# Hybrid decoder layer on one core: the opening rebuilt (how the conditioning row is spread, how the first scale is formed, which tiles start the first projection, and in which order the first loads stand)

## The chip, the cores and the metric

The kernel runs on one core of a Trainium2 chip. The metric is the device time of one execution in microseconds (us); the median of three runs is given. The core's engines run their own queues in order and wait for each other by semaphores: PE multiplies matrices, ACT (ScalarE) and DVE (VectorE) work on tiles in SBUF and PSUM, POOL does little here, and SP issues all the loads. A row "PEld" in the profile is PE loading the stationary operand.

## The reference

One layer (BATCH 1, SEQ 256, D 2048) of a decoder with two token mixers:

```python
mod = silu(c) @ ada_w + ada_b              # 6 vectors of 2048: sh1, sc1, g1, sh2, sc2, g2
h = rms_norm(x, norm1_g) * (1 + sc1) + sh1
proj = h @ w_in + b_in                     # 22 slabs of 512 columns: u, lru_gate, q, k, v, two gates
...                                        # conv + RG-LRU on u and lru_gate, windowed attention on q, k, v
merged = sigmoid(gA) * (y_lru @ w_lru_out) + sigmoid(gB) * (y_attn @ w_attn_out)
x = x + g1 * (merged @ w_o)
h2 = rms_norm(x, norm2_g) * (1 + sc2) + sh2
x = x + g2 * ((silu(gate) * up) @ w_ffn_out)
out = rms_norm(x, final_g)
```

All inputs and the output are float32. A column of `h` (a "k-tile" is 128 of the 2048 rows of the contraction) can be formed only when the shift and the scale of that k-tile are known, and each of these is a dot product of `silu(c)` with 128 columns of `ada_w`.

## The kernel before

**Layout.** Activations are kept transposed: 16 k-tiles of 128 partitions by 256 tokens. `xT` holds x in four tiles of four k-tiles. Weights come from memory in "items" of up to two k-tiles by 512 columns (128x1024 f32, 512 KB; a single k-tile is 256 KB).

**Three products for one.** For most products a weight `raw` is split into a high part (`hi`, a CAST to fp32r on ACT, L274) and a low part (`lo = raw - hi`, a subtraction on DVE, L286); h is split in the same way into `h_hi` and `h_lo` (both in `h_both`). `mm3` (L319 to L321) issues hi\*hi, hi\*low and low\*hi. One k-tile of one 512-column slab is 4 blocks of 128 columns, so 12 matmuls of 128x256; this is called a unit below. `raw` has 5 buffers, `hi` 4 (`N_HI`), `lo` 3 (`N_LO`): the `lo` of item i cannot be written before PE has finished item i-3, the `hi` of item i not before PE has finished item i-4.

**Modulation.** For k-tile kt and vector m, 128 rows of transposed `ada_w` come as two halves of 128x1024 (`aw`). A fused multiply-and-sum on DVE (L406) multiplies each with `crow`, the row silu(c) on all 128 partitions. A short instruction (L414) finishes the scale. So k-tile kt of h takes four halves (2 MB and four L406), then `x_norm` (L433), then on ACT `hx` (L445) and the CAST to `h_hi` (L448), then `h_lo` on DVE (L450). The four halves of each k-tile are named aw0, aw1, ... in the order of their loads.

**Opening.** The row c is loaded onto one partition and spread by four matmuls with one row of ones (L162); ACT applies SiLU on the way to `crow`. The scale of k-tile 0 does not go this way: `sum_first` multiplies one column of silu(c) at a time with 128 columns of `ada_w` (`ak`, 8 loads), 16 matmuls that leave one row of 128 values; the row is copied by ACT and turned into a column by a small matmul (`scT`). The sum of squares of x goes from ACT and DVE into four matmuls (`ssc`), a root, a reciprocal, two products with an identity and a matmul (`rx_ps`), so that 1/rms stands in every partition (`rx`). Before all that, four matmuls on ones (`warm`) run on PE.

**First projection.** The slabs of `START` (8 of u and lru_gate, k, v, 4 of q) are done in three pieces (`N_PIECES`): `cuts()` sets for each slab up to which k-tile each piece goes, from a model of when h is there. The first four slabs (`N_F`) go first, k-tile by k-tile, in `add_first` (k-tiles 0 to 2, `K_FIRST`): 12 items of one k-tile each. Then the items of `add_slab` follow, slab by slab.

**What sets the order.** The order within each engine's queue is written by the program itself while it is built. `step(i)` issues the loads up to item i+5, the `hi` up to item i+3, the `lo` up to item i+2, then the products of item i, then as much side work (`hmod` makes k-tiles of h, `ada` makes modulation columns) as a planner's clock says fits under them; the clock starts at `T_START` and counts 2.62 us for 1024 columns on PE, 1.13 on DVE, 0.95 on ACT. When the products of an item need a k-tile that is not there yet, `hact` issues the missing side work on the spot, behind what already stands in the queues.

Of the kernel before, what the change touches and what calls it, by code (L numbers as in the profile page):

```python
# [65 lines left out]
def hybrid_layer(  # L66
    ctx: ExitStack, tc, vecs, x_t, c_row, ada_k, ada_t, ada_g, w_in, bv_row, bm_row, bg_row, lru_w, w_lru, w_att, w_o,
# [45 lines left out]
    c_ = [b4(f"c{i}", F32, (CH,)) for i in range(2)]  # L113
    for i in range(2):
        nc.sync.dma_start(c_[i][0:1, :], c_row[:, i * CH:(i + 1) * CH])
# [11 lines left out]
    first = []  # L127

    def load_first(n):
        for i in range(len(first), n):  # L130
# [1 line left out]
            nc.sync.dma_start(first[i][:, :2 * N_K * P], ada_k[i])
# [13 lines left out]
    sc_ps = wtile("sc_ps")[:, 0:2, :].rearrange("p j n -> p (j n)")  # L146

    def sum_first(a, b):
        for k in range(a, b):
# [1 line left out]
            nc.tensor.matmul(
                sc_ps[0:1, :N_K * P], lhsT=cact[:, k:k + 1], rhs=first[k // 2][:, c0:c0 + N_K * P],
                start=k == 0, stop=k == NK - 1,
            )
# [4 lines left out]
    def c_rows(a, b):
        for i in range(a, b):  # L160
            ps = mtile(f"c_ps{i}")
            nc.tensor.matmul(  # L162
                ps, lhsT=ones[0:1, :], rhs=c_[i // 2][0:1, (i % 2) * 512:(i % 2 + 1) * 512], start=True, stop=True
            )
            nc.scalar.activation(crow[:, i * 512:(i + 1) * 512], ps, AF.Silu)
            free(m=1)
# [268 lines left out]

    def modulated():
        for kt in range(NK):
            q = kt // 4
# [5 lines left out]
            tj = sp.tile([P, S], F32, tag="t2", name=f"hx{kt}")
            nc.scalar.activation(  # L445
                tj, xT[q][:, kt % 4, :], AF.Identity, bias=modc[:, 0, kt:kt + 1], scale=modc[:, 1, kt:kt + 1],
            )
            nc.scalar.copy(h_hi[:, kt, :], tj)  # L448
# [911 lines left out]
```

## Time and profile before

| | |
|---|---|
| median of 3 runs | 1603.84 us (1596.5, 1605.55, 1603.84) |
| the profiled execution | 1602.11 us, span of the profile 1600.3 us |
| PE busy | 98% of the span |
| DVE, ACT busy | 70%, 48% |
| mean granted PE clock | 0.995 of full speed |
| memory traffic | 399.36 MB, mean 250 GB/s |

The span is the time between the first and the last instruction of the profiled execution. A matmul's recorded time overlaps the next one's, so the pace of PE is read from the starts, not from the durations. PEclk is the granted share of the PE clock. In the queue of an engine an "idle before" names what ended the wait.

### The profile page before, as it was taken

What the parts mean: (1) busy time and instruction counts of PE and PEld (TensorE: products, weight loads), DVE (VectorE), ACT (ScalarE), POOL (GpSimd) and SP (SyncE); (2) the same over time, 40 slices, a digit from 0 to 9 for tenths busy, and PEclk for the clock granted to TensorE, in tenths of its full rate; (3) what the DMA queues carried; (4) which work ended last, traced back from release to release, by engine and by line L of the source; (5) the groups of instructions that cost most, each with busy time, mean ns of one, the idle gap of its engine ahead of it and who ended that gap; (6) DMA issues with size and microseconds to landing.
All of it is one profiled execution on the core that took longest, in us unless ns stands there. A gap on an engine that the chain in (4) does not pass through costs nothing.

```text
span 1600.3 us, 22537 instructions
## 1 busy us (share of the span) xinstructions
PE 1573.8 (98%) x8522; PEld 1359.8 (85%) x8522; DVE 1124.5 (70%) x1426; ACT 768.7 (48%) x973; POOL 4.8 (0%) x9
## 2 busy tenths in 40 slices
PE   8999999999999999999999999999999999999997
PEld 6999999998878787878998878888888888888886
DVE  5789988989988888888657877445454554444465
ACT  4754444485865455443446434444444444333343
POOL 0000000000000000000000000000000000000000
PEclk9999999999999999999999999999999999999999
DMA  8998998766677888999866899666666666665553
GB/s 295 329 348 305 337 337 285 262 222 212 224 272 256 269 270 298 333 310 318 279 185 219 305 326 327 178 190 191 186 193 187 188 194 224 235 196 190 194 197 118
DMA packets 113730, 399.36 MB, mean 250 GB/s; under 512 B 12627, under 2 KB 13779, under 8 KB 113237
## 3 DMA queue, kind: packets, MB, share of 16 engines
q1 hardware_dynamic: 113622, 397.93, 74.9%
q8 instruction: 66, 1.08, 0.3%
q14 instruction: 42, 0.34, 0.1%
HBM read 393.69 MB, written 4.19 MB: 249 GB/s over the span
## 4 chain that ended last, share of the span: by engine, by line
PE 86%; DMA 7%; DVE 4%; issue 2%; ACT 1%; SPq 0%; DVEq 0%; ACTq 0%
PE pf L1085 11%; PE wi L321 6%; PE wi L320 6%; PE wi L319 6%; PE fg L319 4%; PE fg L320 4%; PE fg L321 4%; PE fu L320 4%; PE fu L319 4%; PE fu L321 4%; PE pl L1085 3%; DMA aw<-in_ada_g_dram 3%; DMA aw<-in_ada_t_dram 2%; PE wo L319 2%; PE wo L320 2%; PE wo L321 2%
## 5 line engine op out<-in xcount | busy, mean ns | idle before, releaser
L274 ACT CAST hi<-raw 128x1024 fp32r<-128x1024 f32 (+1 forms) x552 | 564.9, 1028 | 756.4 <-PE pf L1085 109.8
L286 DVE TENSOR_TENSOR lo<-raw,hi 128x1024 fp32r<-128x1024 f32 (+1 forms) x552 | 654.9, 1192 | 361.4 <-PE pf L1085 95.2
L321 PE MATMUL wi<-h_both,lo 128*128 128x256 f32 x784 | 222.1, 283 | 1.0 <-DVE lo L286 1.0
L319 PE MATMUL wi<-h_both,hi 128*128 128x256 f32 x784 | 222.6, 284 | 0.0
L320 PE MATMUL wi<-h_both,hi 128*128 128x256 f32 x784 | 221.9, 283 | 0.0
L321 PEld LDWEIGHTS wi<-h_both,lo 128*128 128x128 f32 x784 | 150.5, 192 | 1.4 <-DVE lo L286 1.4
L320 PEld LDWEIGHTS wi<-h_both,hi 128*128 128x128 f32 x784 | 150.5, 192 | 0.2
L319 PEld LDWEIGHTS wi<-h_both,hi 128*128 128x128 f32 x784 | 150.5, 192 | 0.2
L319 PE MATMUL fg<-hi,h_both 128*128 128x512 f32 x352 | 139.5, 396 | 0.0
L320 PE MATMUL fu<-lo,h_both 128*128 128x512 f32 x352 | 137.0, 389 | 0.3 <-DVE lo L286 0.3
L321 PE MATMUL fg<-hi,h_both 128*128 128x512 f32 x352 | 137.1, 390 | 0.0
L320 PE MATMUL fg<-lo,h_both 128*128 128x512 f32 x352 | 137.1, 389 | 0.0
L321 PE MATMUL fu<-hi,h_both 128*128 128x512 f32 x352 | 136.9, 389 | 0.0
L319 PE MATMUL fu<-hi,h_both 128*128 128x512 f32 x352 | 136.9, 389 | 0.0
L406 DVE CUSTOM_DVE_ANT_0 aw<-aw,crow,modc 128x1024 f32<-128x1024 f32 x79 | 100.9, 1281 | 15.0 <-DMA aw<-in_ada_t_dram 14.9
L406 DVE CUSTOM_DVE_ANT_0 aw<-aw,crow,vec 128x1024 f32<-128x1024 f32 x79 | 100.9, 1279 | 14.6 <-DMA aw<-in_ada_t_dram 14.5
L1085 PE MATMUL pf<-hi,fh 128*128 128x512 f32 x264 | 88.5, 389 | 0.0
L1085 PE MATMUL pf<-lo,fh 128*128 128x512 f32 x264 | 88.4, 389 | 0.0
L1085 PE MATMUL pf<-hi,fl 128*128 128x512 f32 x264 | 88.4, 389 | 0.0
L319 PEld LDWEIGHTS fg<-hi,h_both 128*128 128x128 f32 x352 | 66.1, 188 | 14.4 <-issue 1.0
L320 PEld LDWEIGHTS fu<-lo,h_both 128*128 128x128 f32 x352 | 66.1, 188 | 14.4 <-DVE lo L286 0.7
L320 PEld LDWEIGHTS fg<-lo,h_both 128*128 128x128 f32 x352 | 66.1, 188 | 14.2 <-issue 1.0
(233 smaller groups left out, 2617.2 us busy)
## 6 DMA issues: line engine op xcount, KB each, us to landing
raw<-in_w_f_dram SPq DMA_DIRECT2D x176, 512.0 KB, 3.6
raw<-in_w_in_dram SPq DMA_DIRECT2D x160, 512.0 KB, 6.9
aw<-in_ada_t_dram SPq DMA_DIRECT2D x158, 512.0 KB, 5.9
raw<-in_w_f2a_dram SPq DMA_DIRECT2D x44, 512.0 KB, 4.1
raw<-in_w_lru_dram SPq DMA_DIRECT2D x32, 512.0 KB, 6.8
raw<-in_w_att_dram SPq DMA_DIRECT2D x32, 512.0 KB, 7.1
raw<-in_w_o_dram SPq DMA_DIRECT2D x32, 512.0 KB, 4.0
aw<-in_ada_g_dram SPq DMA_DIRECT2D x32, 512.0 KB, 5.6
```

The costliest lines, as they stand in the source:

```text
L274: nc.scalar.copy(hi[:, :cols], live[i][0][:, :cols])
L286: nc.vector.tensor_tensor(lo[:, :cols], raw[:, :cols], f32(hi[:, :cols]), op=ALU.subtract)
L319: nc.tensor.matmul(ps, lhsT=lh, rhs=rh, start=start, stop=False, skip_group_check=True)
L320: nc.tensor.matmul(ps, lhsT=lh, rhs=rl, start=False, stop=False, skip_group_check=True)
L321: nc.tensor.matmul(ps, lhsT=ll, rhs=rh, start=False, stop=stop, skip_group_check=True)
L406: nc.vector.tensor_tensor_reduce(out=r, in0=r, in1=crow[:, j * CH:(j + 1) * CH], op0=ALU.mult, op1=ALU.add, scale=1.0, scalar=dst if j els ...
L1085: nc.tensor.matmul(fin[t, n], lhsT=l[:, rows(t)], rhs=w[:, c0:c0 + 512], start=kt == 0 and k == 0, stop=kt == (EARLY if (t, n) == (1, 3) e ...
```

## The change

It replaces the opening and leaves the rest of the program as it is, except where the new opening moves the planner's order.

1. c is no longer loaded as a row. DVE multiplies the identity with four columns of silu(c) at a time (dense 128x512 blocks with 128x128 diagonals), and four matmuls with a full 128x128 of ones spread them; DVE copies the results to `crow`. ACT has no part in it any more.
2. `ada_k` comes in two loads of 512 KB instead of eight of 128 KB, and `sum_first` uses the column of silu(c) broadcast to 128 columns as the stationary operand, so that every partition gets the whole row; a fused multiply-and-sum with the identity then takes the diagonal as the column. `sc_row` and `scT` go.
3. The squares of each x tile are added up by themselves and handed on; the matmuls `ssc` take two tiles instead of all.
4. `warm` matmuls stand in three places: 6 at the start, 2 and 6 around `rx_ps`.
5. The first four slabs take k-tiles 0 and 1 (`K_FIRST` 2) as plain f32 products of the raw weights (`wf`) with `hx`, 16 matmuls for each k-tile, without hi and low parts. k-tile 0 of h is made on DVE straight from PSUM.
6. The loads: modulation halves aw0, aw1, then the four f32 weights of k-tile 0, then aw2 to aw5, then those of k-tile 1, and only then the items.
7. `T_START` goes from (23, 27) to (31, 32); the cuts of the pieces follow from `K_FIRST`.

```diff
-N_PIECES, N_F, K_FIRST = 3, 4, 3
+N_WARM = (6, 2, 6)
+N_PIECES, N_F, K_FIRST = 3, 4, 2
-T_START = (23.0, 27.0)
+T_START = (31.0, 32.0)
...
-    c_ = [b4(f"c{i}", F32, (CH,)) for i in range(2)]
-    for i in range(2):
-        nc.sync.dma_start(c_[i][0:1, :], c_row[:, i * CH:(i + 1) * CH])
...
+    first = [b4(f"ak{i}", F32, (NK // 2, P)) for i in range(2)]
+    for i in range(2):
+        nc.sync.dma_start(first[i], ada_k[i])
...
+    crow = ap_.tile([P, D], F32, tag="pal", name="crow")
+    for i in range(4):
+        cs = slice(i * 512, (i + 1) * 512)
+        nc.vector.tensor_tensor(
+            crow[:, cs].rearrange("p (j n) -> p j n", n=P), ident.unsqueeze(1).broadcast_to([P, 4, P]),
+            cact[:, 4 * i:4 * i + 4].unsqueeze(2).broadcast_to([P, 4, P]), op=ALU.mult,
+        )
+        c_ps.append(mtile(f"c_ps{i}"))
+        nc.tensor.matmul(c_ps[i], lhsT=ones, rhs=crow[:, cs], start=True, stop=True)
...
     def sum_first(a, b):
         for k in range(a, b):
             nc.tensor.matmul(
-                sc_ps[0:1, :N_K * P], lhsT=cact[:, k:k + 1], rhs=first[k // 2][:, c0:c0 + N_K * P],
+                sc_ps, lhsT=cact[:, k:k + 1].broadcast_to([P, P]), rhs=first[k // 8][:, k % 8, :],
                 start=k == 0, stop=k == NK - 1,
             )
...
+    def products(self, kt, n):
...
+        for f in range(4):
+            nc.tensor.matmul(
+                self.banks[n][f // 2][:, f % 2, :], lhsT=self.w[kt, n][:, f * P:(f + 1) * P], rhs=hx[kt],
+                start=kt == 0 and f % 2 == 0, stop=kt == K_FIRST - 1, skip_group_check=True,
+            )
...
     fetch_to(2)
-    upto("load", do_load, N_F)
+    begin.load(0)
     fetch_to(6)
-    upto("load", do_load, AHEAD - 1)
+    begin.load(1)
...
+    nc.vector.tensor_tensor_reduce(
+        out=sqx[0][:, 1, 0:P], in0=sc_ps, in1=ident, op0=ALU.mult, op1=ALU.add, scale=1.0,
+        scalar=vec[:, V_ADA + NK:V_ADA + NK + 1], accum_out=dst,
+    )
+    nc.vector.scalar_tensor_tensor(dst, dst, 1.0, vec[:, V_N1:V_N1 + 1], op0=ALU.add, op1=ALU.mult)
     until({(0, 0)})
+    x0 = xT[0][:, 0, :]
+    nc.vector.scalar_tensor_tensor(x0, x0, dst, rx_ps, op0=ALU.mult, op1=ALU.mult)
+    hx[0] = sp.tile([P, S], F32, tag="t2", name="hx0")
+    nc.vector.tensor_scalar(hx[0], x0, modc[:, 0, 0:1], None, op0=ALU.add)
+    for n in range(N_F):
+        begin.products(0, n)
...
+    until({(0, 1), (1, 1)})
+    hmod.advance(True)
+    for n in range(N_F):
+        begin.products(1, n)
+    upto("load", do_load, AHEAD - 1)
+    hmod.finish_to(lambda: 1 in h_done)
+    upto("hi", do_hi, 1)
+    upto("lo", do_lo, 1)
+    for n in range(2):
+        begin.post(n)
+    upto("hi", do_hi, 2)
+    upto("lo", do_lo, 2)
     clock.update(pe=T_START[0], dve=T_START[1], act=T_START[1])
+    for n in range(2, N_F):
+        begin.post(n)
-    for i in range(N_F + 2, len(items)):
+    for i in range(len(items)):
         step(i)
```

`post` copies a finished slab with its bias from PSUM to `acc`, four ACT instructions each. From here on the items after the f32 products are numbered from 0 in the changed kernel (hi0, lo0, ...); in the kernel before, items 0 to 11 are those of `add_first`. The cuts of the first piece were k-tiles 3 3 3 3 3 3 3 4 4 5 5 6 6 7 for the 14 slabs of `START`, and are 2 2 2 2 2 3 3 3 4 4 4 5 5 6.

**ACT, where the first four slabs leave PSUM.** Before, between `hx2` and the second slab's copies (acc0, acc4, acc1, acc5 are the four slabs, w0 to w3 their PSUM tiles):

```order
L445 ACTIVATE hx2_383<-xT0_89,modc_160 128x256
L448 CAST h_both_161<-hx2_383 128x256
L274 CAST hi9_389<-raw9_343 128x512
L274 CAST hi10_411<-raw10_362 128x512
L274 CAST hi11_429<-raw11_387 128x512
L478 ACTIVATE acc0_450<-w0_0_263,vec_87 128x256 x2
L478 ACTIVATE acc0_450<-w0_1_264,vec_87 128x256 x2
L274 CAST hi12_457<-raw12_409 128x1024
L478 ACTIVATE acc4_474<-w1_0_282,vec_87 128x256 x2
L478 ACTIVATE acc4_474<-w1_1_283,vec_87 128x256 x2
```

Now, from the CAST of k-tile 1 of h on:

```order
L456 CAST h_both_155<-hx1_269 128x256
L274 CAST hi0_303<-raw0_260 128x1024
L495 ACTIVATE acc0_307<-w0_0_233,vec_83 128x256 x2
L495 ACTIVATE acc0_307<-w0_1_234,vec_83 128x256 x2
L495 ACTIVATE acc4_312<-w1_0_239,vec_83 128x256 x2
L495 ACTIVATE acc4_312<-w1_1_240,vec_83 128x256 x2
L274 CAST hi1_317<-raw1_262 128x1024
L495 ACTIVATE acc1_321<-w2_0_245,vec_83 128x256 x2
L495 ACTIVATE acc1_321<-w2_1_246,vec_83 128x256 x2
L495 ACTIVATE acc5_326<-w3_0_251,vec_83 128x256 x2
L495 ACTIVATE acc5_326<-w3_1_252,vec_83 128x256 x2
L274 CAST hi2_333<-raw2_295 128x512
```

Before, the copies alternate with CASTs, the first behind `hx2`; now all 16 copies stand in one stretch with `hi0`, `hi1` and `hi2`, and `hx2` comes after them (behind `hi5`).

**DVE, the four halves of k-tile 2 of h.** In the changed kernel (aw6 to aw9 are those halves; the short read of the sum that follows each L406 is left out here and below):

```order
L286 TENSOR_TENSOR lo2_337<-raw2_295,hi2_333 128x512
L433 TENSOR_TENSOR xT0_85<-xT0_85,rx_225 128x512
L406 ISA aw6_271,modc_154<-aw6_271,crow_117,vec_83 128x1024
L286 TENSOR_TENSOR lo3_378<-raw3_297,hi3_335 128x1024
L406 ISA aw7_273,modc_154<-aw7_273,crow_117,vec_83 128x1024
L286 TENSOR_TENSOR lo4_415<-raw4_299,hi4_376 128x512
L406 ISA aw8_275,modc_154<-aw8_275,crow_117,modc_154 128x1024
L406 ISA aw9_277,modc_154<-aw9_277,crow_117,modc_154 128x1024
L414 SCALAR_TENSOR_TENSOR modc_154<-modc_154,vec_83 128x1
L445 TENSOR_TENSOR h_both_155<-hx2_420,h_both_155 128x256
```

Before, the same four halves stood like this:

```order
L286 TENSOR_TENSOR lo5_325<-raw5_246,hi5_303 128x512
L406 ISA aw6_252,modc_160<-aw6_252,crow_123,vec_87 128x1024
L406 ISA aw7_254,modc_160<-aw7_254,crow_123,vec_87 128x1024
L286 TENSOR_TENSOR lo6_347<-raw6_248,hi6_323 128x512
L406 ISA aw8_256,modc_160<-aw8_256,crow_123,modc_160 128x1024
L286 TENSOR_TENSOR lo7_366<-raw7_250,hi7_345 128x512
L406 ISA aw9_258,modc_160<-aw9_258,crow_123,modc_160 128x1024
L414 SCALAR_TENSOR_TENSOR modc_160<-modc_160,vec_87 128x1
L433 TENSOR_TENSOR xT0_89<-xT0_89,rx_223 128x512
L450 TENSOR_TENSOR h_both_161<-hx2_383,h_both_161 128x256
```

They stood behind and between `lo5`, `lo6` and `lo7`, and the first products with k-tile 2 were those of item 8; now they stand behind and between `lo2`, `lo3` and `lo4`, and the first products with k-tile 2 are those of item 2.

**DVE, the last halves of k-tile 3 of h.** In the changed kernel (aw13 is the last half, item 8 the first that uses k-tile 3):

```order
L286 TENSOR_TENSOR lo8_536<-raw8_441,hi8_501 128x1024
L286 TENSOR_TENSOR lo9_561<-raw9_473,hi9_534 128x1024
L406 ISA aw12_382,modc_154<-aw12_382,crow_117,modc_154 128x1024
L286 TENSOR_TENSOR lo10_596<-raw10_499,hi10_559 128x1024
L406 ISA aw13_479,modc_154<-aw13_479,crow_117,modc_154 128x1024
L414 SCALAR_TENSOR_TENSOR modc_154<-modc_154,vec_83 128x1
L445 TENSOR_TENSOR h_both_155<-hx3_605,h_both_155 128x256
L286 TENSOR_TENSOR lo11_639<-raw11_532,hi11_594 128x1024
```

Before (aw13 is the last half here too, item 19 the first that uses k-tile 3):

```order
L286 TENSOR_TENSOR lo17_621<-raw17_525,hi17_584 128x512
L286 TENSOR_TENSOR lo18_644<-raw18_559,hi18_619 128x1024
L406 ISA aw13_448,modc_160<-aw13_448,crow_123,modc_160 128x1024
L414 SCALAR_TENSOR_TENSOR modc_160<-modc_160,vec_87 128x1
L406 ISA aw14_531,modc_160<-aw14_531,crow_123,vec_87 128x1024
L286 TENSOR_TENSOR lo19_679<-raw19_582,hi19_642 128x1024
L286 TENSOR_TENSOR lo20_707<-raw20_617,hi20_677 128x1024
L450 TENSOR_TENSOR h_both_161<-hx3_695,h_both_161 128x256
```

Before, the last half stood behind `lo18`, one item ahead of the first use; now it stands behind `lo10`, two items after it.

More of the change, by code (lines that the diff above doesn't have):

```diff
@@ L140, in hybrid_layer, with keep_warm @@
-    for _ in range(N_WARM):
-        nc.tensor.matmul(warm[:, 0:P], lhsT=ones, rhs=ones, start=True, stop=True)
-    free(m=1)
+    eps_t = const.tile([P, 1], F32, name="eps_t")
+    nc.vector.memset(eps_t, EPS)
+    ident = const.tile([P, P], F32, name="ident")
+    make_identity(nc, ident)
+    def keep_warm(n):
+        warm = mtile("warm")
+        for _ in range(n):
+            nc.tensor.matmul(warm[:, 0:P], lhsT=ones, rhs=ones, start=True, stop=True)
+        free(m=1)
+    keep_warm(N_WARM[0])
@@ L157, in hybrid_layer @@
-    sqx = [b4(f"sqx{q}") for q in range(4)]
[L159 to L166, printed above, removed]
+    early_root()
+    crow = ap_.tile([P, D], F32, tag="pal", name="crow")
+    c_ps = []
+    for i in range(4):
[6 more added lines that the diff above has]
+        nc.tensor.matmul(c_ps[i], lhsT=ones, rhs=crow[:, cs], start=True, stop=True)
@@ L434, in x_norm, with h_f32, h_low @@
         normed.update(range(kt, kt + n))
-    def modulated():
-        for kt in range(NK):
-            q = kt // 4
+    hx = {}
+    def h_f32(kt):
+        tj = hx[kt] = sp.tile([P, S], F32, tag="t2", name=f"hx{kt}")
+        nc.scalar.activation(
+            tj, xT[kt // 4][:, kt % 4, :], AF.Identity, bias=modc[:, 0, kt:kt + 1], scale=modc[:, 1, kt:kt + 1],
+        )
+    def h_low(kt):
+        nc.vector.tensor_tensor(h_lo[:, kt, :], hx[kt], f32(h_hi[:, kt, :]), op=ALU.subtract)
+        h_done.add(kt)
+    def modulated():
+        for kt in range(2):
+            if kt == 1:
+                yield 0.28, 0
+                x_norm(1, 1)
+                yield 0, 0.6, 0, 0, lambda: {(0, 1), (1, 1)} <= cols_done
+                h_f32(1)
+            yield 0, 0.45
+            nc.scalar.copy(h_hi[:, kt, :], hx[kt])
+            yield 0.33, 0
+            h_low(kt)
+        for kt in range(2, NK):
             if kt not in normed:
-                n = 1 if kt < 2 else 4 - kt % 4
+                n = 4 - kt % 4
                 yield 0.28 * n, 0
@@ L443, in modulated @@
             yield 0, 0.9, 0, 0, lambda: {(0, kt), (1, kt)} <= cols_done
[L444 to L448, printed above, removed]
+            h_f32(kt)
+            nc.scalar.copy(h_hi[:, kt, :], hx[kt])
             yield 0.33, 0
-            nc.vector.tensor_tensor(h_lo[:, kt, :], tj, f32(h_hi[:, kt, :]), op=ALU.subtract)
-            h_done.add(kt)
+            h_low(kt)
         free(b4=4)
@@ L1232, in hybrid_layer @@
     free(m=1)
-    sum_first(N_SUM, NK)
-    sc_row = sp.tile([1, N_K * P], F32, tag="t2", name="sc_row")
-    nc.scalar.copy(sc_row, sc_ps[0:1, :N_K * P])
-    scT = mtile("scT")
-    for kt in range(N_K):
-        nc.tensor.matmul(
-            scT[:, kt:kt + 1], lhsT=sc_row[0:1, kt * P:(kt + 1) * P], rhs=ones[0:1, 0:1],
-            start=kt == 0, stop=True, skip_group_check=True,
-        )
-    free(b4=NK // 2)
+    sum_first(NK // 2, NK)
+    keep_warm(N_WARM[1])
     def until(cols):
@@ L1250, in hybrid_layer @@
     nc.vector.reciprocal(rc, rc)
-    for t in range(2):
-        nc.vector.tensor_scalar(sqx[3][:, 2, rows(t)], ident, rc[:, t:t + 1], None, op0=ALU.mult)
+    diag = sqx[0][:, 2, :]
+    nc.vector.tensor_scalar(diag[:, rows(0)], ident, rc[:, 0:1], None, op0=ALU.mult)
+    nc.scalar.activation(diag[:, rows(1)], ident, AF.Copy, scale=rc[:, 1:2])
     rx_ps = mtile("rx_ps")[:, 0:S]
-    nc.tensor.matmul(rx_ps, lhsT=ones, rhs=sqx[3][:, 2, :], start=True, stop=True)
+    nc.tensor.matmul(rx_ps, lhsT=ones, rhs=diag, start=True, stop=True)
```

142 lines of the change are left out of this document (54 added, 88 removed).

## The prediction, made before the changed kernel was run

> **What bounds the kernel now.** The page's busy line first:
>
> ```profile
> PE 1573.8 (98%) x8522; PEld 1359.8 (85%) x8522; DVE 1124.5 (70%) x1426; ACT 768.7 (48%) x973; POOL 4.8 (0%) x9
> ```
>
> PE leaves 26 us of 1600.3 free, so an opening can be worth only what PE waits or runs slowly early on. Next PE's timeline of the opening, which shows when products start and where PE stands still; then busy time and granted clock by stretches, with PE's waits from 50.79 to 363 as the last line (us in total, times, longest):
>
> ```profile
> start us, us, engine line op out<-in xcount [idle before <-releaser]
> 3.06 7.19 PE L162 MATMUL c_ps<-c,ones 1*128 1x512 f32 x8
> 12.01 3.57 PE L151 MATMUL sc_ps<-ak,cact 128*1 128x128 f32 x16 [1.76 <-DMA ak<-in_ada_k_dram]
> 15.51 1.87 PE L1226 MATMUL ssc<-ones,sqx 128*128 128x1 f32 x8
> 17.30 3.53 PE L151 MATMUL sc_ps<-ak,cact 128*1 128x128 f32 x16
> 21.49 0.70 PE L1254 MATMUL rx_ps<-sqx,ones 128*128 128x256 f32 x2
> 24.44 0.58 PE L319 MATMUL w<-h_both,hi 128*128 128x256 f32 x1 [2.25 <-ACT h_both L448]
> 40.85 0.28 PE L321 MATMUL w<-h_both,lo 128*128 128x256 f32 x1
> 42.63 0.38 PE L319 MATMUL w<-h_both,hi 128*128 128x256 f32 x1 [1.50 <-ACT h_both L448]
> 48.04 0.28 PE L320 MATMUL w<-h_both,hi 128*128 128x256 f32 x1
> 50.79 0.28 PE L319 MATMUL wi<-h_both,hi 128*128 128x256 f32 x1
> ```
>
> ```profile
> core 0: us, PE busy (x) PEld busy (x) DVE busy (x) ACT busy (x) POOL busy (x), PEclk, DMA share, GB/s
> 2.00:12.00 10.00, 8.25 (x14) 3.35 (x13) 1.23 (x1) 4.23 (x8) 0.00 (x0) 1.00 0.91 309
> 24.44:30.85 6.41, 6.41 (x29) 6.24 (x30) 6.31 (x11) 2.12 (x4) 0.00 (x0) 0.50 0.80 251
> 40.97:42.63 1.66, 0.16 (x2) 0.00 (x1) 0.56 (x2) 1.05 (x3) 0.00 (x0) 1.00 0.75 217
> 44.50:47.90 3.40, 3.40 (x19) 3.40 (x18) 3.35 (x6) 3.15 (x7) 0.00 (x0) 0.51 0.96 286
> 60.00:363.00 303.00, 302.18 (x2408) 297.32 (x2407) 269.83 (x399) 164.04 (x219) 2.32 (x2) 1.00 0.86 301
> PE wi L321 <- DVE lo L286: 1.0, 2, 0.8
> ```
>
> Products start at 24.44; 6.41 us pass at half clock; PE stands still for 1.66 us before k-tile 2; 3.40 us at half clock follow; at 50.79 twelve units are done. From there to 363 PE loses 1.0 us. PE is the bound there, with DVE behind it at 270 of 303 us. So what the opening leads or lags by at 50.79 reaches the end, neither caught up nor grown, unless the new order makes later waits; code behind the first projection is the same. From 48.04 to 50.79 there are 23 steps of 0.1196 us: a unit takes 1.43 us.
>
> **Start to the first product.** The prices: two lines of the chain for f32 products, groups of DVE and of ACT by form (count, then busy us and mean ns), and five lines of the timelines of DVE, ACT and SP:
>
> ```profile
> 302.01 1.73 PE lr L658 x8
> 521.13 1.72 PE o L782 x4
> L406 DVE CUSTOM_DVE_ANT_0 aw<-aw,crow,modc 128x1024 f32<-128x1024 f32 x9 | 11.5, 1279 | 0.0
> L286 DVE TENSOR_TENSOR lo<-raw,hi 128x1024 fp32r<-128x1024 f32 x9 | 11.0, 1223 | 5.5 <-ACT hi L274 5.0 <-issue 0.3
> L286 DVE TENSOR_TENSOR lo<-raw,hi 128x512 fp32r<-128x512 f32 x15 | 10.1, 688 | 1.1 <-ACT hi L274 0.8 <-PE w L321 0.2
> L433 DVE TENSOR_TENSOR xT<-xT,rx 128x256 f32<-128x256 f32 x2 | 0.8, 422 | 3.0 <-ACT rx L1256 3.0
> L414 DVE SCALAR_TENSOR_TENSOR modc<-modc,vec 128x1 f32<-128x1 f32 x3 | 0.5, 155 | 0.0
> L1252 DVE TENSOR_SCALAR sqx<-ident,rc 128x128 f32<-128x128 f32 x2 | 0.5, 284 | 0.1
> L274 ACT CAST hi<-raw 128x1024 fp32r<-128x1024 f32 x9 | 9.4, 1061 | 3.8 <-DMA raw<-in_w_in_dram 3.8
> L274 ACT CAST hi<-raw 128x512 fp32r<-128x512 f32 x16 | 9.4, 620 | 5.8 <-DMA raw<-in_w_in_dram 3.3 <-DVE lo L286 1.5 <-PE wi L320 1.0
> L445 ACT ACTIVATE hx<-xT,modc 128x256 f32<-128x256 f32 x4 | 2.4, 599 | 7.2 <-DVE xT L433 6.9 <-DVE modc L1262 0.2
> L448 ACT CAST h_both<-hx 128x256 fp32r<-128x256 f32 x4 | 1.6, 405 | 0.1
> 27.36 1.28 DVE L406 CUSTOM_DVE_ANT_0 aw<-aw,crow,vec 128x1024 f32<-128x1024 f32 x1
> 28.56 1.28 DVE L406 CUSTOM_DVE_ANT_0 aw<-aw,crow,modc 128x1024 f32<-128x1024 f32 x1
> 49.35 1.58 ACT L478 ACTIVATE acc<-w,vec 128x256 f32<-128x256 f32 x4
> 0.74 0.63 SPq L115 DMA_DIRECT2D c<-in_c_row_dram  x2
> 3.71 8.21 SPq L132 DMA_DIRECT2D ak<-in_ada_k_dram  x8
> ```
>
> An f32 matmul leaves two records: 4 of 128x256 take 1.73 us, 0.433 each; 2 of 128x512 take 1.72, 0.86 each. The c_ps of the opening, four of 1x512, took 1.80 each: half speed, though the clock column says 1.00 there; I go by the durations. Back to back, instructions overlap a little: the two L406 rows of 1.28 start 1.20 apart, and I take some 0.08 off each mean in a row of work.
>
> Hidden ahead of `sc_ps`, whose data came at 12.01: the row c (two issues, 0.63 us of SP, go), eight `ak` issues of 8.21 us that become two, ACT's four SiLU copies, which become four products and four copies of 128x512 on DVE (about 0.69 each; DVE's time ahead of 12 was idle but for 1.23), and the first warm matmuls. The bytes ahead of `ak` are the same x, so 12.0 stays. The cover is that load; if it came 5 us earlier, DVE's eight instructions, 5.5 us, would be next. The loads behind it are 7 MB up to the last half of k-tile 1, which at the 309 GB/s of the second row is 22.7 us, plus 2 for the start: early enough below. POOL gets nothing.
>
> From 12.0, `sc_ps`, `ssc` and `sc_ps` take 3.57+1.87+3.53 = 9.0 as before; so 21.0 at the old speed. At full speed it would be 16.5, and some 17 with the squares and the root to wait for. I take 18.5, between the ends and nearer to the fast one, since 14 small matmuls and four dense blocks of 128x512 with all 128 rows now stand ahead of them, where the old c_ps had one row. Then the diagonal, an operation that the trace lacks (0.28 as L1252, a DVE instruction of the same 128x128; at most 1.28 as L406, the same kind at eight times the width; 0.4 taken, nearer to the same size), 0.16 for the scale, the other half's L406 1.28 and two 128x256 instructions of 0.42: 2.7, first product at 21.2 (19.8 to 23.7 with 17 and 21.0 for the start). Before: 24.44. So 3.2 us are gained here, and the slow 6.41 behind 24.44 may fall away too.
>
> **The f32 k-tiles.** 16 x 0.433 = 6.9 us each, 28.2 and 35.1. For k-tile 1 DVE needs 0.42 + 0.42 + 4 x 1.20 (the step between the two L406 rows) + 0.16, ACT 0.60, handovers 0.4: 28.0, just covered. The split products of the same eight units are 96 x 0.1196 = 11.5 at full clock, so f32 costs 2.4 more; before, they took 40.97 - 24.44 = 16.5 in fact, so the gain here is in slow clock and in waits for `lo`, not in arithmetic. Items 0 and 1 complete the twelve units: 48 x 0.1196 = 5.7, at 40.9; their hi and lo, on ACT and DVE from 28.5 on, are ready by then. Lead over 50.79: 9.9.
>
> **The wait for k-tile 2.** By the order above, ACT does, after h of k-tile 1 at 28.1, its CAST 0.41, hi0 and hi1 (0.98 each, back to back), 16 copies (step 1.58/4, 0.37 with overlap) 5.9, hi2 0.6: 37.0. DVE then stands before lo2, and from 37.0 runs lo2 0.69, `x_norm` 0.6, aw6 1.20, lo3 1.15, aw7 1.28, lo4 0.6, aw8 and aw9 2.56, L414 0.16: 45.2. ACT's `hx`, CAST and handovers 1.2: 46.4. PE, done at 40.9, waits 5.5. Queued behind that on DVE and ACT are only later parts of the same chain, and SP's loads wait for buffers that PE frees. Even without ACT's delay lo4 needs the buffer of lo1, free when PE ends item 1; lo4, aw8, aw9, L414 and 1.2 follow: 4.6 at least. Lead left: 4.4.
>
> **The clock.** 1.66 us of standing cost 3.40 us at 0.51 (rows above): 1.7 us. Behind 5.5 us I take 2.5, midway between that 1.7 and half of the 6.41 behind 24.44, 3.2, where PE had stood 2.25. The Trainium skill ("TensorE: Matmul & The Clock Gate", "What's actually happening") says that one busy window of about 3.4 us brings the full clock; 3.40 after 40.97 agrees, 6.41 and the 7.19 us of c_ps at half speed do not.
>
> **The waits for k-tiles 3 and 15.** Before, their `hx` came ahead of need:
>
> ```profile
> 65.12 0.60 ACT L445 ACTIVATE hx<-xT,modc 128x256 f32<-128x256 f32 x1
> 236.05 1.05 ACT L274 CAST hi<-raw 128x1024 fp32r<-128x1024 f32 x1 [2.26 <-PE wi L320]
> 237.01 0.59 ACT L445 ACTIVATE hx<-xT,modc 128x256 f32<-128x256 f32 x1
> ```
>
> Now aw13 stands behind lo10, which needs lo7's buffer, free at the end of item 7; item 8 needs k-tile 3 in its second half. From that end: 1.2 + 1.28 + 0.16 + 0.6 + 0.41 + 0.2 = 3.9, less three matmuls that can go, 0.36: 3.5, with 2.5 of clock. `hx` of k-tile 15 stands behind the CAST of item 76, which needs the end of item 72, while item 73 uses k-tile 15: 1.05 + 0.6 + 0.41 + 0.1 - 0.36 = 1.8, plus some slack 2.0, with 1.7 of clock. Each of the three restarts also waits some 0.3 for `h_lo` (0.42 on DVE like the 128x256 of L433, while three matmuls can go ahead): 0.9. Nearest in the old run to these two waits are the 1.0 us in all of the last line above, so 0.5 to 4 is the span for each.
>
> **Sum.** 4.4 - 2.5 (clock) - 6.0 (k-tile 3) - 3.7 (k-tile 15) - 0.9 = -8.7: later by 8.7, against the profiled execution's 1602.11 1610.8. The median shown is 1.7 above that execution; 1603.84 + 8.7 = 1612.5.
>
> **The rivals.** 0.5%, about what a measurement here can tell from no change, is 8.0 us: 1595.8 and 1611.9.
> - B: the clock holds through the waits. Without 2.5 + 2.5 + 1.7 it is 1605.8. For it: c_ps, dense now, and long f32 products may keep it up. Against: the 0.51 behind a gap of 1.66. By the Trainium skill (same page, "HAM oscillation — how this bites in real kernels") only gaps above some 3.4 us cost clock; the 1.66 row speaks against it; by it the 2.0 us wait alone would be free: 1610.8.
> - C, faster: the halves of k-tile 2 run ahead. If DVE is not held by hi2, k-tile 2 comes within 13 us of 28.1, and PE has no wait there. It decides from 41: then the lead is 9.9, less 6.0 if k-tile 3 is late still and 3.7 if k-tile 15 is: about 1604; with PE's queue then earlier and these two on time, 1594. The floor of 4.6 speaks against.
> - D: the opening does not do what it says: the f32 products run at half rate, as c_ps did. One k-tile so, 6.9 more, while the wait behind shrinks by part of that: 1616; both, 1621.
>
> **Chances.** Forecast 0.53 (1607 to 1618, by 19.8 to 23.7 and the clock's 1.7 to 3.2, three times), with 0.30 of it above 1611.9; B 0.20; C with the faster end 0.15; D 0.12. Faster 0.15, same 0.23 + 0.20 = 0.43, slower 0.30 + 0.12 = 0.42. The range for 8 in 10 takes B in and part of D: 1601 to 1619; the faster cases and both k-tiles at half rate stay out. The likeliest's time stands on the border between same and slower.
>
> **What would show it.** PE's first product at about 21 and its last f32 one near 35; PE waits for `h_both` at about 41, 62 to 66 and 245, of 5.5, 3.5 and 2.0 us, each with 0.5 in the clock column behind; DVE idle before lo2 for `hi`. Wrong it is, if the wait at 41 is below 3, if the clock stays 1.00 behind it, or if the first product comes before 19 or after 24.

## The result, and the profile after

| | before | changed |
|---|---|---|
| median of 7 runs, us | 1599.71 (1596.5 to 1605.55) | 1610.88 (1609.65 to 1613.9) |
| profiled execution, us | 1602.11 | 1612.98 |
| span of the profile, us | 1600.3 | 1611.2 |
| mean granted PE clock | 0.995 | 0.989 |

The ratio is 1.0064 (95% interval 1.0048 to 1.008): slower by about 10 us. The prediction was 1612.5, with 1601 to 1619 as its range. The result lay nearest to the forecast case; rivals B, C and D did not come. The 1612.5 stood on a median of 1603.84 for the kernel before, where the seven executions here give 1599.71. As a lag, 8.7 us were forecast and 11.2 measured between the medians (10.3 by the ratio), so that the absolute times agree better than the lags is luck.

The page of the changed kernel, its busy line and the clock in 40 slices:

```profile
PE 1578.3 (98%) x8508; PEld 1367.3 (85%) x8508; DVE 1126.9 (70%) x1429; ACT 766.5 (48%) x959; POOL 3.0 (0%) x9
PEclk8899999999999999999999999999999999999999
```

Two slices are below 9 now, the two that hold the first 80 us. PE's timeline there (start us, us, instruction, idle before and what ended it), the answer to the one shown of before:

```profile
4.29 3.72 PE L156 MATMUL c_ps<-crow,ones 128*128 128x512 f32 x8 [0.31 <-DVE crow L151]
11.86 3.75 PE L186 MATMUL sc_ps<-ak,cact 128*128 128x128 f32 x16 [3.84 <-DMA ak<-in_ada_k_dram]
15.40 1.71 PE L1247 MATMUL ssc<-ones,sqx 128*128 128x1 f32 x8
16.97 3.76 PE L186 MATMUL sc_ps<-ak,cact 128*128 128x128 f32 x16
23.38 1.99 PE L537 MATMUL w<-hx,wf 128*128 128x256 f32 x8
37.10 0.47 PE L319 MATMUL wi<-h_both,hi 128*128 128x256 f32 x1
48.33 0.58 PE L319 MATMUL wi<-h_both,hi 128*128 128x256 f32 x1 [5.12 <-ACT h_both L466]
67.10 0.58 PE L319 MATMUL wi<-h_both,hi 128*128 128x256 f32 x1 [3.36 <-ACT h_both L466]
249.72 0.39 PE L319 MATMUL wi<-h_both,hi 128*128 128x256 f32 x1 [2.05 <-ACT h_both L466]
```

The dense blocks do what the change says: four c_ps take 3.72 us in place of 7.19. But then PE stands for 3.84 us until `ada_k` has come, and `sc_ps`, `ssc` and `sc_ps` take as long as before. The f32 products run from 23.38 to 37.10, and three waits for `h_both` follow, those of k-tiles 2, 3 and 15. The same places in stretches, with PE's busy time and, third from the right, the granted clock:

```profile
core 0: us, PE busy (x) PEld busy (x) DVE busy (x) ACT busy (x) POOL busy (x), PEclk, DMA share, GB/s
4.29:8.00 3.71, 3.71 (x8) 1.45 (x8) 3.67 (x7) 1.71 (x4) 0.00 (x0) 1.00 0.96 326
11.86:20.60 8.74, 8.74 (x41) 8.74 (x42) 3.65 (x9) 0.66 (x2) 0.00 (x0) 0.50 1.03 407
23.38:37.10 13.72, 13.72 (x64) 12.09 (x65) 8.53 (x14) 7.89 (x17) 0.00 (x0) 1.00 1.03 405
43.05:48.33 5.28, 0.16 (x3) 0.00 (x1) 4.18 (x9) 2.05 (x3) 0.00 (x0) 0.72 0.97 340
48.33:52.10 3.77, 3.77 (x16) 3.60 (x17) 0.96 (x2) 1.39 (x4) 0.00 (x0) 0.50 0.88 355
67.10:71.30 4.20, 4.20 (x18) 4.03 (x19) 0.40 (x1) 0.84 (x2) 0.00 (x0) 0.50 1.02 412
249.72:254.00 4.28, 4.21 (x20) 4.01 (x21) 2.31 (x10) 0.00 (x0) 0.54 (x2) 0.60 0.93 288
```

The f32 products had the full clock; behind each wait the clock is 0.5 to 0.6 for some 4 us. PE's waits from 20 to 380 in sum (us, times, longest), where before had, from 50.79 to 363, 1.0 us of them:

```profile
PE wi L319 <- ACT h_both L466: 10.5, 3, 5.1
PE wi L321 <- DVE lo L286: 1.7, 2, 1.2
PE wi L320 <- DVE lo L286: 0.3, 1, 0.3
PE wi L319 <- DVE acc L484: 0.2, 1, 0.2
```

And why k-tile 2 was late, two rows of DVE and two of ACT:

```profile
39.28 0.69 DVE L286 TENSOR_TENSOR lo<-raw,hi 128x512 fp32r<-128x512 f32 x1 [2.21 <-ACT hi L274]
47.05 0.16 DVE L414 SCALAR_TENSOR_TENSOR modc<-modc,vec 128x1 f32<-128x1 f32 x1
38.56 1.63 ACT L274 CAST hi<-raw 128x512 fp32r<-128x512 f32 x2
47.24 0.60 ACT L440 ACTIVATE hx<-xT,modc 128x256 f32<-128x256 f32 x1 [3.07 <-DVE modc L414]
```

hi2 comes at 38.56, behind the sixteen copies; lo2 waits for it at the head of DVE's queue, the four halves stand behind lo2, and the scale is complete at 47.05, four microseconds after PE ran dry at 43.05.

To follow the loss, two points far behind the opening serve in all that follows: the start of the products of `wgl` (PE has then done the same work in every kernel here) and that of `fu`, in the feed-forward part. First before, then the changed kernel (x count: min/median/max ns, first to last start):

```profile
L319 PE MATMUL wgl<-hi,h_both x128: 388/389/580, 363.2 to 456.7; 128*128 128x512 f32 x128
L319 PE MATMUL fu<-hi,h_both x352: 388/389/389, 878.5 to 1350.7; 128*128 128x512 f32 x176
```

```profile
L319 PE MATMUL wgl<-hi,h_both x128: 387/389/580, 374.9 to 470.9; 128*128 128x512 f32 x128
L319 PE MATMUL fu<-hi,h_both x352: 388/389/395, 890.5 to 1361.4; 128*128 128x512 f32 x176
```

Later by 11.7 at the first and by 12.0 at the second. The end of the span is later by 10.9.

### The profile page after: what moved, and what is told of

Its sections match the earlier page's. It is cut to its first block, busy times and chain, and to the rows that moved or that the text cites. A ratio compares the mean times of both kernels' runs of the same rounds, so it can differ in the third digit from the quotient of the medians.

```text
span 1611.2 us, 22443 instructions
## 1 busy us (share of the span) xinstructions
PE 1578.3 (98%) x8508; PEld 1367.3 (85%) x8508; DVE 1126.9 (70%) x1429; ACT 766.5 (48%) x959; POOL 3.0 (0%) x9
## 4 chain that ended last, share of the span: by engine, by line
PE 84%; DMA 8%; DVE 4%; ACT 2%; issue 1%; SPq 0%; DVEq 0%; ACTq 0%
PE pf L1106 11%; PE wi L320 6%; PE wi L319 6%; PE wi L321 6%; DMA aw<-in_ada_g_dram 4%; PE fg L319 4%; PE fg L320 4%; PE fu L319 4%; PE fu L321 4%; PE fu L320 4%; PE fg L321 4%; PE pl L1106 3%; DMA aw<-in_ada_t_dram 2%; PE wo L319 2%; PE wo L321 2%; PE wo L320 2%
## 5 line engine op out<-in xcount | busy, mean ns | idle before, releaser
L319 PE MATMUL wi<-h_both,hi 128*128 128x256 f32 x800 | 230.1, 288 | 10.7 <-ACT h_both L466 10.5
L321 PE MATMUL wi<-h_both,lo 128*128 128x256 f32 x800 | 228.9, 286 | 1.7 <-DVE lo L286 1.7
L320 PE MATMUL wi<-h_both,hi 128*128 128x256 f32 x800 | 229.1, 286 | 0.1
L319 PEld LDWEIGHTS wi<-h_both,hi 128*128 128x128 f32 x800 | 155.9, 195 | 11.7 <-ACT h_both L466 11.1
L321 PEld LDWEIGHTS wi<-h_both,lo 128*128 128x128 f32 x800 | 155.9, 195 | 2.3 <-DVE lo L286 2.3
L320 PEld LDWEIGHTS wi<-h_both,hi 128*128 128x128 f32 x800 | 155.9, 195 | 0.9 <-DVE h_both L445 0.6
L406 DVE CUSTOM_DVE_ANT_0 aw<-aw,crow,vec 128x1024 f32<-128x1024 f32 x79 | 100.9, 1281 | 15.3 <-DMA aw<-in_ada_t_dram 15.3
L406 DVE CUSTOM_DVE_ANT_0 aw<-aw,crow,modc 128x1024 f32<-128x1024 f32 x79 | 100.9, 1280 | 13.5 <-DMA aw<-in_ada_t_dram 13.2
```

The costliest lines, as they stand in the source:

```text
L319: nc.tensor.matmul(ps, lhsT=lh, rhs=rh, start=start, stop=False, skip_group_check=True)
L320: nc.tensor.matmul(ps, lhsT=lh, rhs=rl, start=False, stop=False, skip_group_check=True)
L321: nc.tensor.matmul(ps, lhsT=ll, rhs=rh, start=False, stop=stop, skip_group_check=True)
L406: nc.vector.tensor_tensor_reduce(out=r, in0=r, in1=crow[:, j * CH:(j + 1) * CH], op0=ALU.mult, op1=ALU.add, scale=1.0, scalar=dst if j els ...
```

## The experiments

Besides the changed kernel, twelve others were run. Times are compared as ratios to the kernel before, in runs on the same chip; the two points are those of each kernel's one profiled execution, less the 363.2 and 878.5 of before. One execution is a single draw. The opening of the changed kernel stands unaltered in e1 to e4 and e9, and its first product came at 23.38, 20.95, 22.64, 22.36, 22.65 and 23.23 us in those six. From the start of `fu` to the end of the span the kernels other than e8 took between 718.3 and 721.8 us. So 2 to 3 us in one execution, at the two points or at the end, need not be the edit's.

| kernel | median, us | ratio to before (95%) | wgl | fu |
|---|---|---|---|---|
| changed | 1610.88 | 1.0064 (1.0048 to 1.0080) | +11.7 | +12.0 |
| e1: k-tile 2 ahead | 1604.53 | 1.0019 (1.0006 to 1.0033) | +2.6 | +2.7 |
| e2: later k-tiles ahead | 1604.06 | 1.0019 (1.0006 to 1.0031) | +2.5 | +4.1 |
| e3: e1 and e2 | 1600.94 | 1.0005 (0.9991 to 1.0019) | -1.7 | +1.0 |
| e4: warm matmuls in the waits | 1608.55 | 1.0049 (1.0034 to 1.0064) | +6.1 | +9.7 |
| e5: warm matmuls ahead of sc_ps | 1612.66 | 1.0081 (1.0061 to 1.0100) | +7.5 | +12.7 |
| e6: no warm matmuls | 1612.93 | 1.0079 (1.0060 to 1.0097) | +7.6 | +11.9 |
| e7: e3 and e5 | 1600.82 | 0.9997 (0.9982 to 1.0011) | -2.7 | -0.2 |
| e8: e7, four `lo` buffers | 1682.75 | 1.0522 (1.0499 to 1.0545) | +6.1 | +69.5 |
| e9: twelve halves less | 1607.28 | 1.0042 (1.0024 to 1.0060) | +11.7 | +12.8 |
| e10: e5 and e9 | 1609.32 | 1.0049 (1.0031 to 1.0066) | +7.5 | +6.3 |
| e11: before, more warm | 1601.93 | 0.9993 (0.9977 to 1.0009) | -1.3 | +1.9 |
| e12: e7, hi2 ahead too | 1598.86 | 0.9984 (0.9968 to 0.9999) | -5.6 | +1.1 |

### e1: k-tile 2 ahead

```diff
     upto("lo", do_lo, 1)
+    ada.advance(True)        # three times
     for n in range(2):
         begin.post(n)
     upto("hi", do_hi, 2)
     upto("lo", do_lo, 2)
+    until({(0, 2), (1, 2)})
+    hmod.finish_to(lambda: 2 in h_done)
```

> The four halves of k-tile 2 and its h are put ahead of lo2 on DVE, and ahead of hi2 and of the last eight copies on ACT; all else as in the changed kernel. My theory (the queues' order makes the wait at 43 us): PE's wait of 5.1 us before item 2 falls below 1, the clock stays 1.00 behind it, and the waits for k-tiles 3 and 15 stay as they are (3.4 and 2.0), since they hang on PE's own progress: 5.1 + 1.9 of clock + 0.3, some 7 us below the changed kernel's 1610.9, 1604. Rival (the halves land too late, and loads set k-tile 2): a wait of 3 us or more stays, with DVE idle on loads of aw, and the time is within 2.5 us of 1610.9.

As expected in the main, 1604.5. The wait of 5.12 us is gone, and so the loads are not what held k-tile 2. What is late next is hi2, now behind `hx` and eight copies; k-tiles 3 and 15 still wait:

```profile
42.33 0.39 PE L319 MATMUL wi<-h_both,hi 128*128 128x256 f32 x1 [1.55 <-ACT hi L274]
58.10 0.38 PE L319 MATMUL wi<-h_both,hi 128*128 128x256 f32 x1 [1.67 <-ACT h_both L466]
239.97 0.39 PE L319 MATMUL wi<-h_both,hi 128*128 128x256 f32 x1 [2.04 <-ACT h_both L466]
```

The wait for k-tile 3 halved, from 3.36 to 1.67, which had been expected to stay; that DVE is less behind here is a likely reason, not a tested one. Of the 9.1 us gained at wgl, 2.4 are the earlier first product of this execution (20.95 for 23.38), which the edit does not touch; 6.7 are left, near the 7 expected and the 7.2 of the ratios (0.0045 of 1600).

### e2: later k-tiles two items ahead

```diff
     for i in range(len(items)):
+        for kt in uses.get(i + 2, ()):      # the k-tiles that item i + 2 multiplies
+            if kt > 2:
+                until({(0, kt), (1, kt)})
+                hmod.finish_to(lambda: kt in h_done)
         step(i)
```

> From k-tile 3 on, the modulation columns and h of a k-tile are put into the queues two items ahead of the item that uses it; the opening and k-tile 2 stay as in the changed kernel. My theory: the waits of 3.4 us (k-tile 3) and 2.0 us (k-tile 15) fall below 0.5 each, the clock stays 1.00 behind both, and the time falls by 3.4 + 2.1 + 2.0 + 1.7 and some 0.5 for h_lo, 9 to 10 us: about 1601. Rival (DVE is short there): PE waits for lo of items 9 to 11 and 73 to 76 in place of h, and the time stays above 1607.

The waits for k-tiles 3 and 15 are gone; 0.66 us for `lo` is left in the place of the first. At the start of wgl 9.2 us are gained, as expected (0.7 of them by a first product at 22.64); by the ratios 7.2 us.

### e3: both

> The edits of e1 and e2 together. My theory: the three waits are the whole of the loss, and the two gains add up: 16 us below the changed kernel, 1594 to 1596, about 5 us faster than the kernel before. Rival (later waits of other stages take the lead back, or the opening itself gains nothing): no better than the kernel before, 1600 or more.

The three waits are the whole of the loss, that holds: with them gone the changed kernel is where the kernel before is. The gains do not add up, though: 9.4 us by the ratios, against 7.2 and 7.2. At the start of wgl 13.4 us are gained, 1.0 of them by a first product at 22.36. PE meets the next one in line there, six waits for `lo` of 4.4 us in all in place of the changed kernel's 1.7; and from wgl to fu it takes 2.7 us more than before. So the rival is right on the size.

### e4: the clock priced alone

```diff
         while kt not in h_done:      # in hact
+        if kt not in h_done and kt in {2: 20, 3: 13, 15: 8}:
+            keep_warm({2: 20, 3: 13, 15: 8}[kt])     # ahead of the loop
```

> The order stays; PE only gets 20, 13 and 8 matmuls on ones (128x128, f32) to do where it waits for k-tiles 2, 3 and 15. This prices the clock alone. My theory: PE starts on each of the three k-tiles at the same distance as before, but PEclk stays 1.00 behind it: 1.9 + 2.1 + 1.7, some 5.7 us below the changed kernel, 1605. Rival (the clock is not kept by such matmuls, or falls for another reason): 0.5 stays in the column behind the waits, time within 2 us of 1610.9 or above.

The clock behind the three waits, one stretch for each:

```profile
47.60:52.00 4.40, 4.33 (x34) 4.13 (x35) 1.63 (x2) 2.08 (x5) 0.00 (x0) 1.00 0.77 302
64.86:69.00 4.14, 4.06 (x27) 3.64 (x28) 1.39 (x2) 1.82 (x5) 0.00 (x0) 1.00 1.03 406
245.20:250.00 4.80, 4.70 (x37) 4.50 (x38) 3.88 (x12) 1.05 (x1) 0.54 (x2) 1.00 0.92 300
```

1.00 in all three, in place of 0.50, 0.50 and 0.60. At the start of wgl PE is 5.6 us earlier than in the changed kernel, 0.7 of which it had from a first product at 22.65; the terms of the clock in the prediction are right in kind, and 4.9 in place of 6.7 in size. But by the ratios, whose intervals overlap, only 2.4 us arrive at the end, and in the profiled execution 3.3 us of the 5.6 are gone by the start of fu.

### e5 and e6: the warm matmuls of the opening

In e5 `keep_warm(14)` stands behind the four c_ps; in e6 `N_WARM` is (0, 0, 0).

> The changed kernel with 14 more matmuls on ones behind the four c_ps, so that PE has work while it waits 3.84 us for the loads of ada_k; the order is otherwise the same. My theory (sc_ps and ssc run at half speed in the changed kernel only since that wait drops the clock): sc_ps, ssc, sc_ps take about 4.7 us in place of 8.7, the first f32 product comes at about 19.5 in place of 23.4, the three waits for h stay (5.1, 3.4, 2.0), since k-tile 2's chain moves with the rest: 3.5 us below the changed kernel, 1607. Rival (the second half of ada_k or the squares set the pace, or the two halves for k-tile 0 do): the first product at 22 or later and less than 1.5 us gained.

> The changed kernel without any of its 14 matmuls on ones. My theory: c_ps start at half clock (some 7 us for four in place of 3.7), which the wait for ada_k hides; the first f32 product comes where it did, but at half clock for about 3 us more, so 1.5 to 2 us later at the end of the f32 products, and as much in the end: 1612 to 1613. Rival (sc_ps and rx_ps bring the clock up by themselves): no difference, within 1 us of 1610.9.

e5, two rows of PE's timeline, and then e6, two:

```profile
12.21 1.95 PE L187 MATMUL sc_ps<-ak,cact 128*128 128x128 f32 x16
19.58 4.58 PE L538 MATMUL w<-hx,wf 128*128 128x256 f32 x20 [0.42 <-DVE hx L1285]
```

```profile
4.22 6.58 PE L156 MATMUL c_ps<-crow,ones 128*128 128x512 f32 x8 [4.22 <-DVE crow L151]
12.28 2.02 PE L186 MATMUL sc_ps<-ak,cact 128*128 128x128 f32 x16 [1.47 <-DMA ak<-in_ada_k_dram]
```

e5 did in the opening what was expected, to a tenth: sc_ps at full speed, first product at 19.58, three waits unchanged (5.15, 3.36, 2.05), 4.2 us ahead of the changed kernel at wgl. e6 turned out the other way: without warm matmuls the c_ps take 6.58 us, end at 10.8 and leave a gap of only 1.47, behind which sc_ps run at full speed (2.02), and the first product comes at 20.55. That is 2.8 us ahead of the changed kernel's profiled execution, but only 0.4 ahead of the earliest of the six with the same opening (20.95 in e1). So the warm matmuls of the change did not help here; that they do harm, by letting the c_ps end early into a longer gap, is not shown by one execution of e6.

Neither is faster at the end. e5 and e6 are 4.2 and 4.1 us ahead at wgl, and 0.7 behind and 0.1 ahead at fu. Here a statement of the prediction falls: that what the opening leads by at 50.79 reaches the end. What takes the lead back is PE waiting for DVE between wgl and fu. Three of these waits (us, times, longest), first in the changed kernel, then in e5:

```profile
PE mt L857 <- DVE gate L874: 3.7, 3, 2.1
PE pt L792 <- DVE sc L786: 0.7, 1, 0.7
PE wa L320 <- DVE lo L286: 0.5, 1, 0.5
```

```profile
PE mt L858 <- DVE gate L875: 5.8, 3, 2.4
PE pt L793 <- DVE sc L787: 2.5, 1, 2.5
PE wa L321 <- DVE lo L287: 1.5, 1, 1.5
```

All of PE's waits in that stretch, every one for DVE, sum to 5.6 us in the changed kernel, 10.6 in e5 and 10.5 in e6, and the stretch takes 515.6, 520.5 and 519.6 us. The last modulation half is summed from 776.6, 775.9 and 776.5 us on in the three, so DVE is less than 1 us earlier there, although PE was 4 us ahead at wgl.

### e7: e3 with e5

> The edits of e3 and e5 together: k-tile 2 ahead, later k-tiles two items ahead, 14 warm matmuls in the wait for ada_k. My theory: e5's gain at the start comes on top of e3, 1597 to 1598, the first of these kernels clearly below the one before (1600.5). Rival (in e3 PE already waits for lo on DVE at six places, and DVE is next in line, so an earlier start of PE turns into longer waits for lo): within 1.5 us of e3's 1600.9, with waits for lo above e3's 4.4 us.

The rival's time: 1600.8, as e3. Its cause did not come: the waits for `lo` ahead of wgl fell to 3.3 us from 4.7, where it expected more. Instead PE waits 2.11 us for hi2 at 41.2, and a first f32 product at 19.28, 3.1 us earlier than in e3, is worth 1.0 us at wgl.

### e8: four buffers for lo

```diff
-AHEAD, N_HI, N_LO, N_ADA, N_B4 = 6, 4, 3, 2, 25
+AHEAD, N_HI, N_LO, N_ADA, N_B4 = 6, 4, 4, 2, 24
```

> The kernel of e7 with four buffers for lo in place of three (N_LO 4; one of the 25 shared tiles goes for the room), so that each lo is issued one item earlier on DVE. My theory (e3's six waits for lo, 4.4 us and a slow restart each, come from lo standing behind modulation halves with only three buffers): these waits fall below 1.5 us between 37 and 363, and 3 to 4 us are gained on e7. Rival (DVE has no time left there, or the tile that is gone delays the side work): the waits stay or move behind 363, and nothing is gained.

Far worse, and not for the reason that was asked for: the waits for `lo` before 363 did fall to 2.1 us, though 4.0 for `h_both` and 2.6 for `hi` came, but the modulation is put off, the last half is summed at 893 (776 in the changed kernel, 764 in e7), and PE pays behind wgl. The shared tile that is gone is the likely cause. PE's largest wait:

```profile
PE wo L323 <- DVE lo L288: 22.4, 8, 14.2
```

Two things were changed at once, so it does not tell what four buffers alone would do.

### e9 and e10: is it the modulation halves that take PE's lead back?

```diff
-    ada = Side(ada_cols(cols, halves), 3)
+    ada = Side(ada_cols(cols[:-3], halves), 3)     # and no loads for these columns
```

> The changed kernel without the last 12 of its 158 modulation halves (their loads and their multiply-and-sums; those columns are only the bias, so the output is not the reference's). It is the base for e10. My theory (between 470 and 890 PE is held by what DVE does with modulation halves as their loads come, which ends at 776 in the changed kernel, in e5 and in e6 alike): the waits of PE for gate and sc in that stretch (4.4 us) shrink, the first product with w_o moves from 768.4 to 766 or earlier relative to the same start of wgl, and 1 to 4 us are gained: 1607 to 1610. Rival (PE alone sets the time there): within 1 us of 1610.9.

> e5 (warm matmuls in the wait for ada_k) without the same 12 halves. My theory: with that load off, the 4.2 us that e5 was ahead at the start of wgl are no longer given back before w_f1, so this runs 3 to 4 us below e9, 1604 to 1606. Rival (e5's lead is lost to something other than the modulation halves): within 1 us of e9.

Both kernels leave out the last twelve modulation halves; their columns hold the bias alone. Not settled. By the ratios e9 is 0.0022 below the changed kernel, with intervals that overlap, and e10 is no faster than e9, which speaks for the rival. In the single profiled executions e10 is 6.5 us ahead of e9 at fu, with PE's waits between wgl and fu at 6.0 us for e9's 7.2, which speaks for the theory. But the profiled execution of e9 took 1611.43 us, 4.2 more than its median, and that of e10 1606.54, 2.8 less than its own. That PE waits for DVE in that stretch of e5 is shown above; whether it is the modulation halves that keep DVE there stays open.

### e11: the old opening, only warmer

```diff
-    for _ in range(N_WARM):
-        nc.tensor.matmul(warm[:, 0:P], lhsT=ones, rhs=ones, start=True, stop=True)
+    keep_warm(8)      # and 8 more behind the c_ps, 6 behind rx_ps
```

> The kernel before, with nothing of the change but its warm matmuls: 8 on ones at the start in place of 4, 8 more behind the four c_ps, 6 behind rx_ps. My theory (what the new opening gains is the clock, which is half in the old one up to 30.85): sc_ps, ssc and the first units run at full clock, the first product comes 2 to 4 us earlier than 24.44, its 6.4 us at half clock are gone, k-tile 1 and 2 of h then set the pace, and 3 to 5 us of it are left: 1596 to 1598, the fastest of all. Rival (the narrow c_ps with one row of ones let the clock fall, or lo and h bind at once): within 1.5 us of the kernel before.

No difference from before. PE's timeline of it:

```profile
4.76 7.19 PE L165 MATMUL c_ps<-c,ones 1*128 1x512 f32 x8
11.89 3.78 PE L142 MATMUL warm<-ones 128*128 128x128 f32 x16
15.60 2.10 PE L154 MATMUL sc_ps<-ak,cact 128*1 128x128 f32 x16
```

The sc_ps are at full speed and so are the products from 24.12 on, but the eight warm matmuls delay sc_ps to 15.60, and then h and `lo` set the pace: PE waits 0.92, 1.23 and 1.49 us for `h_both`, and the clock is at half again behind the last two (third figure from the right):

```profile
32.87:36.50 3.63, 3.57 (x14) 3.04 (x15) 3.63 (x6) 1.51 (x3) 0.00 (x0) 0.53 1.00 389
43.30:46.60 3.30, 3.23 (x15) 3.23 (x16) 3.05 (x7) 2.04 (x5) 0.00 (x0) 0.50 1.00 365
```

So the 6.41 us at half clock in the kernel before cost next to nothing: run fast, the same products end in waits for h and `lo` and in slow clock behind these.

### e12: hi2 ahead too

```diff
     until({(0, 2), (1, 2)})
+    upto("hi", do_hi, 4)
+    hmod.advance(True)
+    upto("lo", do_lo, 3)
     hmod.finish_to(lambda: 2 in h_done)
```

> e7 with hi2, hi3 on ACT and lo2 on DVE moved ahead of hx of k-tile 2 (in e7 they stood behind it and behind eight copies, and PE waited 2.1 us for hi2 at 41). My theory: that wait and the slow clock behind it (0.81 to 0.88 from 37 to 48) go, so PE is 3 to 4 us earlier at the start of wgl than in e7 (360.5), about 357; of that, some half is left at the end: 1597 to 1599, faster than the kernel before by 0.1 to 0.3%. Rival (what PE gains before 363 is taken back between 363 and 890, as e5's 4 us were): no difference from e7's 1600.8.

1598.9, ratio 0.9984 (0.9968 to 0.9999): the only one of these kernels whose interval lies below the one before, if barely, and below the changed kernel by 0.8% by the two ratios. One interval of thirteen that misses 1 by 0.0001 is weak evidence for faster than before; faster than the changed kernel is clear. Its two points:

```profile
L321 PE MATMUL wgl<-hi,h_both x128: 387/389/581, 357.6 to 453.7; 128*128 128x512 f32 x128
L321 PE MATMUL fu<-hi,h_both x352: 388/389/390, 879.6 to 1348.4; 128*128 128x512 f32 x176
```

The start of wgl came at 357.6, as expected, 5.6 us ahead of before; at fu nothing of that is left in the profiled execution (1.1 behind). Again PE's waits for DVE between the two points take the lead back: 11.5 us, in a stretch of 522.0. At the end that execution is 2.1 us ahead of the one of before all the same (spans of 1598.2 and 1600.3), and by the ratio 2.6 us are left, about the half that was expected.

## Why the prediction was right, point by point

- **First product: 21.2 forecast, 23.38 measured.** The step "I take 18.5" is the term that was mis-sized: sc_ps ended at 20.7, next to the slow end of 21.0. Dense c_ps did raise the clock, but behind the wait of 3.84 us for `ada_k`, which the c_ps' own speed made longer, it was at half again. How long it stays there differs between executions: e1, with the same opening and a wait of 4.08, had its first product at 20.95. So part of the 2.2 is the draw. That the full-speed end was real is shown by e5, where the wait is filled: 19.58.
- **f32 products: 13.9 forecast, 13.72 measured**, at full clock; rival D is out. Twelve units were done at 43.05 for 40.9, so the lead over 50.79 was 7.7 for 9.9: the 2.2 of the first step.
- **Wait for k-tile 2: 5.5 forecast, 5.12 measured**, by the chain named (hi2 behind the copies, lo2, four halves, `hx`). e1 shows that it was the order: moved ahead, the wait is gone.
- **k-tile 3: 3.5 and 3.36. k-tile 15: 2.0 and 2.05.** e2 takes both away by order alone.
- **The clock: 2.5, 2.5 and 1.7 forecast.** From the windows above 3.77 x 0.50 = 1.9, 4.20 x 0.50 = 2.1 and 4.28 x 0.40 = 1.7, together 5.7; e4, which removes only that, 4.9. Rival B is out: each of the three waits cost clock.
- **The sum: -8.7 forecast.** Measured terms: 7.7 - 5.3 - 1.9 - 3.4 - 2.1 - 2.05 - 1.7 - 0.9 for the restarts, which were not measured apart, and 1.2 for more waits for DVE (`lo`, and 0.2 for `acc`) ahead of wgl than before had, which the prediction did not have: -10.8. At wgl -11.7 was measured; 0.9 is not traced. So the mechanism was the one forecast, and the lag came out larger by the 2.2 of the first product and the 1.2 of waits for DVE, less the 1.2 by which the waits and the clock cost less than forecast.
- **What was wrong and did not show:** "neither caught up nor grown". A lag of 11.7 us at wgl was one of 12.0 at fu, so here it made no difference. A lead, or a smaller lag with the order unchanged, is not kept whole: in their profiled executions e4, e5 and e6 gained 4 to 6 us by wgl and had 2.3, -0.7 and 0.1 of it at fu; e12 lost 6.7. The ratios of e5 and e6, no lower than the changed kernel's, say the same. PE being busy 302 of 303 us before 363 says nothing of the stages behind, and the prediction had looked for PE's waits only up to there.

## What to carry to other kernels

An opening that starts PE sooner also moves the point at which the rest must be ready: read the queues of the engines that make the next inputs (here the order of hi, copies, lo and modulation on ACT and DVE), and count from the last buffer that they need. Through the clock a wait can cost nearly twice its length (2.05 us cost 1.7 more here, 5.12 only 1.9 more, and the 1.55 in e1 nothing more), so look at the granted clock behind each gap in front of a matmul-bound stretch. A lead of one engine is worth what the next bound stage lets through: put a mark behind each stage and see how much of the lead is left there, before adding up gains.
